# Head of the expert search: both token tiles together, parts evicted in pairs, and the next two heads' products ahead of the rest of the first search

## The chip, the cores and the metric

The kernel runs on one core of one Trainium2 chip. The metric is the device time of one execution in microseconds (us); lower is better. The core has a matrix engine (TensorE, PE in the rows), a vector engine (VectorE, DVE), a scalar engine (ScalarE, ACT), GpSimd (POOL), a queue engine (SyncE, SP) and 16 DMA engines. Each engine runs its own instructions in program order and waits on semaphores for the others.

## The reference, cut to what matters

Three blocks run one after the other on x of 256 tokens by 1024 channels, in float32. The second block ends in a product-key expert layer ("peer"), and the change is in its head. For each token and each of 8 heads a query of two 128-wide halves is scored against 128 sub-keys per half. The best 16 of each half form 256 candidate sums, and the best 16 of these name rows of a table: 16 rows for each of 8 heads and 256 tokens.

```
h2 = rmsnorm_2(x, norm2_g[l]) * (1.0 + sc2) + sh2
x = x + g2 * peer(h2, peer_wq[l], peer_subkeys[l], peer_u[l], peer_v[l])

q = (hf @ wq).reshape(T, PEER_HEADS, 2, PEER_DKEY // 2)
sc = jnp.einsum('thpd,pnd->thpn', q, subkeys)
top_v, top_i = lax.top_k(sc, PEER_TOPK)                  # 16 of 128, twice
cand_v = (top_v[:, :, 0, :, None] + top_v[:, :, 1, None, :]).reshape(T, PEER_HEADS, -1)
cand_id = (top_i[:, :, 0, :, None] * PEER_NKEYS + top_i[:, :, 1, None, :]).reshape(T, PEER_HEADS, -1)
best_v, best_j = lax.top_k(cand_v, PEER_TOPK)            # 16 of 256
ids, gates = take_along_axis(cand_id, best_j), softmax(best_v)
a = einsum('td,ted->te', xb, u_tab[ids]); w = gates * gelu(a)
y = einsum('te,ted->td', w, v_tab[ids])
```

The third block that follows (a long convolution and a mixture of experts) needs the whole x that the second block gives.

## The kernel before, in words

The 256 tokens are two tiles of 128 (t = 0, 1). A step n of the expert layer handles one table row per token of one tile: 256 steps, 128 for each tile, 16 for each head. For a step, GpSimd issues an indirect DMA (`refill`) that gathers 128 rows of 2048 floats, u and v side by side, 1 MiB. VectorE forms the dot of u with the token (`dot`), ScalarE makes the weight and a diagonal matrix from it (`weight`), and TensorE adds the weighted v into PSUM (`add`); then the buffer is free and takes the next gather. At the start there are 12 buffers (three in `E0`, four in `G0`, four in `G1`, and the first of `E0` last). A gather needs the ids of its rows, so the first one waits for the first search.

Float32 products are made of three TensorE passes over parts in a shorter format (`mm3`: high by high, low by high, high by low). Weights come by a ring of five 512 KB slots that SyncE fills in order. For each slot ScalarE writes the high part (`whi`) and VectorE the low part (`wlo`), into three buffers of the pool `split_p`; `get` hands out the next pair, and with `k.still` set it splits just one item when none is left. A slot is filled again once its `wlo` is written.

The head of `peer`: the last products of the attention's output projection end, `x_add` adds them to x in four 128 by 512 pieces (the second half g = 1 with its squares on ScalarE), the rows are normalised (`xn`), transposed on TensorE, scaled and shifted into `hfull`, and split into `hT` (high `hT3h`, low `hT3l`). In the kernel before this is done one tile at a time: `norm_rows(0)`, `transposed_rows(0)`, then the products and scores of head 0 for tile 0 (`first_scores(0)`), then `transposed_rows(1)`. Behind these, `quick` finds the best 8 rows of head 0 from the best 8 of each half; `pump(n)` makes n of the 13 pieces into which `choose` cuts the search of one head. `tokens(t)` transposes the tokens back for the dots. `rest` makes the products of heads 3 to 7 between the steps. `heads["ready"]` is the last head whose scores are there. When `rest` is through, `weights_done` swaps the 12 big buffers for 8 others; once all searches are done, four buffers in the tile `early` are added.

The order of the instructions on each engine is that of the code, written by hand; there is no planner.

Of the kernel before, what the change touches and what calls it, by code (L numbers as in the profile page):

```python
# [11 lines left out]
F32 = mybir.dt.float32  # L12
# [5 lines left out]
ALU = mybir.AluOpType  # L18
# [21 lines left out]
class K:  # L40
# [59 lines left out]
    def _process(self, wait=False, lower=None):  # L100

        nc, i = self.nc, self.done
        self._load(i + 1)
        raw, f = self.raw.pop(i), self.items[i][1]
        self.done += 1
        if f is not None:
            f(raw)
            return
        hi = self.split_p.tile([128, 1024], F32R, name="whi")
        lo = self.split_p.tile([128, 1024], F32R, name="wlo")  # L110
        nc.scalar.activation(hi, raw, AF.Copy)  # L111
        self.parts.append((hi, lo))
        if wait:
            return lambda: nc.vector.tensor_sub(lo, raw, hi)
        (lower or nc.vector).tensor_sub(lo, raw, hi)  # L115

# [705 lines left out]
def block2(k, mod, M):  # L822
# [150 lines left out]
    def x_add(g, r, ps):  # L973
        for t in range(2):
            y = sm.tile([128, 512], F32, name="s2", bufs=3)
            nc.vector.scalar_tensor_tensor(y, ps[t], rg[g][:, t:t + 1], g1[:, r * 512:r * 512 + 512], op0=ALU.mult,
                                           op1=ALU.mult)
            xs = x[:, t, r * 512:r * 512 + 512]
            (nc.vector if g and not t else nc.gpsimd).tensor_add(xs, xs, y)
            if g:  # L980
                k.square(t, r, junk)
# [38 lines left out]
    k._process()  # L1020
# [10 lines left out]
def peer(k, mod, pA, normed_at):  # L1031
# [37 lines left out]
    v2 = tk.tile([128, 2], F32, name="vm2")  # L1069

    def norm_rows(t):
        v = v2[:, t:t + 1]
        nc.vector.tensor_add(v, k.ss[:, 0, t:t + 1], k.ss[:, 1, t:t + 1])
        nc.vector.tensor_scalar(v, v, 1.0 / 1024, 1e-6, op0=ALU.mult, op1=ALU.add)
        nc.vector.tensor_scalar_mul(xn[:, t], x[:, t], k.rsqrt(tk, v, 1, f"m2{t}"))

    def transposed_rows(t, warm=0):

        u = slice(t * 128, t * 128 + 128)
        ps = [k.mm() for _ in range(2)]  # L1080
        k.keep_warm(ps[0], warm)
        for c in range(8):
            nc.tensor.transpose(ps[c // 4][:, c % 4 * 128:c % 4 * 128 + 128], xn[:, t, c * 128:c * 128 + 128], k.ident)

        def lower(q):
            c4 = slice(4 * q, 4 * q + 4)
            nc.vector.tensor_sub(hT[1][:, c4, u], hfull[:, c4, u], hT[0][:, c4, u])

        for q in range(2):
            for j in range(4):  # L1090
                c, src = 4 * q + j, ps[q][:, j * 128:j * 128 + 128]
                if j % 2:
                    nc.scalar.activation(hfull[:, c, u], src, AF.Identity, scale=normed_at[0](c), bias=normed_at[1](c))
                else:
                    nc.vector.tensor_scalar(hfull[:, c, u], src, normed_at[0](c), normed_at[1](c), op0=ALU.mult,
                                            op1=ALU.add)
            nc.scalar.activation(hT[0][:, 4 * q:4 * q + 4, u], hfull[:, 4 * q:4 * q + 4, u], AF.Copy)
            if q:
                lower(0)
        lower(1)  # L1100

    def cols_of_rows(w, t, out):

        for c in range(8):
            k.mm3(out, [z[:, c * 128:c * 128 + 128] for z in w], [z[:, c, t * 128:t * 128 + 128] for z in hT], c == 0,
                  c == 7)
# [5 lines left out]
    def half_products(r, ts=(0, 1)):  # L1112
        q, ps = q3, k.mm()
        for n in range(2):
            for t in ts:
                nc.tensor.matmul(ps[:, t * 256 + n * 128:t * 256 + n * 128 + 128], q[:, n, t * 128:t * 128 + 128],
                                 subk[:, n * 128:n * 128 + 128], start=True, stop=True)
        for t in ts:
            nc.scalar.activation(sc[t][:, 2 * r:2 * r + 2], ps[:, t * 256:t * 256 + 256], AF.Copy)

    def first_scores(t):

        u = slice(t * 128, t * 128 + 128)
        p = k.mm()[:, 0:256].rearrange("p (n t) -> p n t", n=2)
        for i in range(2):
            cols_of_rows(first[i], t, p[:, i])
        nc.scalar.activation(q3[:, :, u], p, AF.Copy)
        half_products(0, (t,))


    norm_rows(0)
    transposed_rows(0, warm=44)
    k._process()
    norm_rows(1)
    first = [k.parts.pop(0) for _ in range(2)]
    first_scores(0)
    transposed_rows(1)


# [203 lines left out]
    def choice(n):  # L1343
# [3 lines left out]
        if n == 132:  # L1347
            finish(0)
        refill()


    quick()
    refill()
    tokens(0)
    first_scores(1)
    pump(13)
    refill()
    for r in (1, 2):
        k.later(half_scores, r, k.pair(hT))
    k.settle()  # L1360
    k.settle()
    heads["ready"] = 2
    pump(13)
    refill()
# [32 lines left out]
    tiles = rest()  # L1397
    ahead(0)
    ahead(1)
    for n in range(N):  # L1400
        choice(n)
        if pr is None or n % 4 != 3:
            pump(1)
        refill()

        if tiles is not None:
            if n % 7 == 1 and n < 70:
                next(tiles)
            elif n % 7 in (3, 5) and n > 7:
                k.settle()  # L1410
                if n % 14 == 12:
# [1056 lines left out]
```

## Time and profile before

| | |
|---|---|
| device time, median of 3 runs | 2510.76 us (2506.67, 2510.76, 2510.79) |
| profiled execution: device time / span | 2506.08 us / 2504.3 us |
| TensorE busy (share of the span) | 2067.5 us (83%) |
| VectorE busy | 1281.8 us (51%) |
| ScalarE busy | 773.0 us (31%) |
| GpSimd busy | 320.9 us (13%) |
| DMA, bytes and mean rate | 861.30 MB, 344 GB/s |
| of it by GpSimd's queue (the gathers) | 268.45 MB |

The span is the time from the first to the last instruction of the profiled execution, and 1.8 us lie around it. A busy share is a mean over all three blocks, whose limits differ, so what a change in one stage is worth is read from the rows of that stage.

### The profile page before, as it was taken

The page shows a single profiled execution, that of the slowest core. Times are in us where ns is not written, and L with a number is a line of the kernel's source. Part 1 is how long each engine was busy: PE and PEld are TensorE (multiplying, and loading weights), DVE is VectorE, ACT ScalarE, POOL GpSimd, SP SyncE. Part 2 cuts the span into 40 slices and gives each one's busy share as a digit, 9 for nine tenths or more (in the row PEclk, how much of TensorE's full clock was granted, in tenths as well). Part 3 has the DMA queues.
Part 4 walks back from the last instruction along what each step waited for, and adds up shares of the span by engine and source line. Part 5 has one row for each costly group of instructions (what it writes and reads, how often), then busy time and mean ns, then how long its engine had stood idle before and what let it go on. Part 6 is the DMA issues. An engine that isn't in the chain of part 4 may idle for free. (4 is left out here: it accounts for less than half of the span.)

```text
span 2504.3 us, 30432 instructions
## 1 busy us (share of the span) xinstructions
PE 2067.5 (83%) x11288; PEld 1223.2 (49%) x11288; DVE 1281.8 (51%) x2507; ACT 773.0 (31%) x1670; POOL 320.9 (13%) x314
## 2 busy tenths in 40 slices
PE   9999999999889978988858999877776676666776
PEld 8789899788755523443423997311211111111121
DVE  8987789877678758877845887100000000000001
ACT  5754444446345545554433433000000000000000
POOL 0100000000234333333323230000000000000000
PEclk9999999999699999999999999988788887987788
DMA  7767688775399999999997358999999999999997
GB/s 261 237 213 255 209 303 304 256 249 177 117 397 419 419 419 419 406 420 421 420 419 291 119 169 311 408 418 417 417 417 418 417 417 418 417 417 418 417 417 290
DMA packets 176308, 861.30 MB, mean 344 GB/s; under 512 B 29992, under 2 KB 35296, under 8 KB 107296
## 3 DMA queue, kind: packets, MB, share of 16 engines
q1 hardware_dynamic: 125872, 578.19, 60.1%
q0 software_dynamic: 36864, 268.45, 25.9%
q10 hardware_dynamic: 13424, 12.72, 1.6%
q8 instruction: 89, 1.46, 0.2%
q14 instruction: 59, 0.48, 0.1%
HBM read 858.19 MB, written 1.10 MB: 343 GB/s over the span
## 5 line engine op out<-in xcount | busy, mean ns | idle before, releaser
L115 DVE TENSOR_TENSOR wlo<-ring,whi 128x1024 fp32r<-128x1024 f32 x224 | 277.5, 1243 | 103.7 <-ACT whi L111 102.3
L2110 DVE TENSOR_TENSOR xe<-mm,m 128x256 f32<-128x256 f32 x15 | 6.4, 425 | 604.5 <-PE mm L2108 604.5
L111 ACT ACTIVATE whi<-ring 128x1024 fp32r<-128x1024 f32 x228 | 239.3, 1055 | 163.4 <-PE mm L162 46.1
L2152 PE MATMUL mm<-K,xe 128*32 128x512 f32 x864 | 150.8, 688 | 83.0 <-DMA K<-in_moe_w_dram 82.9
L2152 PE MATMUL mm<-we,xe 128*32 128x512 f32 x864 | 143.7, 758 | 83.2 <-DMA we<-in_moe_w_dram 82.8
L161 PE MATMUL mm<-hTh,whi 128*128 128x256 f32 x608 | 174.8, 287 | 0.8 <-DVE hTl L309 0.8
L163 PE MATMUL mm<-hTh,wlo 128*128 128x256 f32 x608 | 172.8, 284 | 0.1
L162 PE MATMUL mm<-hTl,whi 128*128 128x256 f32 x608 | 172.4, 284 | 0.0
L2173 ACT ACTIVATE he<-mm 128x512 f32<-128x512 f32 x16 | 9.5, 597 | 451.0 <-PE mm L2152 451.0
L1313 ACT ACTIVATE dots<-dots 128x1 f32<-128x1 f32 x256 | 51.7, 202 | 292.1 <-DVE rowsS L1302 67.6
L1324 PE MATMUL ys<-rowsS,diag 128*128 128x512 f32 x240 | 115.3, 621 | 28.9 <-ACT diag L1316 28.8
L2189 ACT ACTIVATE heT<-mm 128x512 f32<-128x512 f32 x16 | 9.6, 597 | 379.9 <-PE mm L2187 369.6
L2255 POOL TENSOR_TENSOR x<-x,zT 128x512 f32<-128x512 f32 x1 | 1.6, 1557 | 963.7 <-ACT x L2254 963.7
L2152 PEld LDWEIGHTS mm<-K,xe 128*32 128x32 f32 x864 | 22.5, 115 | 209.9 <-DMA K<-in_moe_w_dram 194.6
L2219 DVE TENSOR_TENSOR ye<-mm,px_m 128x512 f32<-128x512 f32 x16 | 11.1, 692 | 210.5 <-PE mm L2213 210.5
L161 PEld LDWEIGHTS mm<-hTh,whi 128*128 128x128 f32 x608 | 115.7, 190 | 4.7 <-issue 2.9
L2152 PEld LDWEIGHTS mm<-we,xe 128*32 128x32 f32 x864 | 20.7, 119 | 199.0 <-DMA we<-in_moe_w_dram 179.7
L162 PEld LDWEIGHTS mm<-hTl,whi 128*128 128x128 f32 x608 | 115.3, 190 | 0.6
L163 PEld LDWEIGHTS mm<-hTh,wlo 128*128 128x128 f32 x608 | 115.3, 190 | 0.3 <-DVE wlo L115 0.3
L375 DVE SCALAR_TENSOR_TENSOR mod<-ring,mod_t,mod 128x1024 f32<-128x1024 f32 x84 | 111.2, 1324 | 0.0
L1324 PE MATMUL ys<-early,diag 128*128 128x512 f32 x172 | 84.4, 628 | 27.4 <-ACT diag L1316 27.4
L1316 ACT ACTIVATE diag<-ident,dots 128x128 f32<-128x128 f32 x256 | 102.8, 402 | 12.5 <-PE ys L1324 4.4
(556 smaller groups left out, 4821.4 us busy)
## 6 DMA issues: line engine op xcount, KB each, us to landing
we<-in_moe_w_dram SPq DMA_DIRECT2D x160, 1024.0 KB
K<-in_moe_w_dram SPq DMA_DIRECT2D x122, 1024.0 KB
ring<-in_moe_w_dram SPq DMA_DIRECT2D x100, 512.0 KB
K<-in_moe_w_dram SPq DMA_DIRECT2D x84, 512.0 KB
ring<-in_w_in_dram SPq DMA_DIRECT2D x48, 512.0 KB
ring<-in_ada_w_dram SPq DMA_DIRECT2D x48, 512.0 KB
ring<-in_mod_w_dram SPq DMA_DIRECT2D x48, 512.0 KB
ring<-in_w_qkv_dram SPq DMA_DIRECT2D x24, 512.0 KB
```

What stands on the lines that cost most here:

```text
L111: nc.scalar.activation(hi, raw, AF.Copy)
L115: (lower or nc.vector).tensor_sub(lo, raw, hi)
L161: nc.tensor.matmul(out, lhs[0], rhs[0], start=start, stop=False)
L162: nc.tensor.matmul(out, lhs[0], rhs[1], start=False, stop=False)
L163: nc.tensor.matmul(out, lhs[1], rhs[0], start=False, stop=stop)
L375: nc.vector.scalar_tensor_tensor(z, raw, th[:, ch:ch + 1], z, op0=ALU.mult, op1=ALU.add)
L1313: nc.scalar.activation(g, a, AF.Gelu)
L1316: nc.scalar.activation(diags[n], k.ident, AF.Copy, scale=w)
L1324: nc.tensor.matmul(ys[-1][:, 512 * j:512 * j + 512], d, rows[n][1][:, 1024 + 512 * j:1536 + 512 * j], start=n % 128 == 0, stop=n % 128 == 127)
L2152: nc.tensor.matmul(p[32 * j:32 * j + 32], xe[:, c], w[j], start=c == 0, stop=c == 7)
L2189: nc.scalar.activation(heT, p, AF.Copy)
L2219: nc.vector.tensor_mul(ye, p, m5)
```

## The change

The head handles all 256 tokens at once. `x_add` gives the piece t = 1 to VectorE and t = 0 to GpSimd (before it was the other way round). One `rms_x` serves both tiles; the 16 transposes fill four PSUM banks, and each eviction takes a part of 256 columns where it took 128. The low and high splits are written out in pairs of parts. The two weight items of head 0 are split in two steps: `uppers(2)` lets ScalarE write both high parts early, and `lower()` puts each low part on VectorE at a chosen place. Head 0's products are then one `pair` of 48 TensorE passes with 256 columns (before: 48 passes with 128 columns per tile, at two places). Behind `quick`, the products of heads 1 and 2 come first and the rest of head 0's search (`pump(13)`) after them; the search of head 1 moves into the first seven steps, two pieces a step. `rest` starts one item earlier, its scores count as ready seven steps earlier, and later seven steps of eight carry a piece of search (before: three of four).

```diff
-            (nc.vector if g and not t else nc.gpsimd).tensor_add(xs, xs, y)
+            (nc.vector if g and t else nc.gpsimd).tensor_add(xs, xs, y)
...
     k.rows_part(p3, yT, 3, 4)
-    k._process()
     k.later(x_add, 1, 1, p3)
...
+    def uppers(self, n):
+        self.lowers = [self._process(wait=True) for _ in range(n)]
+    def lower(self):
+        self.lowers.pop(0)()
...
-    norm_rows(0)
-    transposed_rows(0, warm=44)
-    k._process()
-    norm_rows(1)
-    first = [k.parts.pop(0) for _ in range(2)]
-    first_scores(0)
-    transposed_rows(1)
+    k.uppers(2)
+    r = k.rms_x(tk, "m2")
+    for t in range(2):
+        nc.vector.tensor_scalar_mul(xn[:, t], x[:, t], r[:, t:t + 1])
+    ps4 = [k.mm() for _ in range(4)]
+    k.keep_warm(ps4[0], 40)
+    for c in range(8):
+        for t in range(2):
+            o = c % 2 * 256 + t * 128
+            nc.tensor.transpose(ps4[c // 2][:, o:o + 128], xn[:, t, c * 128:c * 128 + 128], k.ident)
+    def full(c, on_dve):
+        src, sc, sh = ps4[c // 2][:, c % 2 * 256:c % 2 * 256 + 256], normed_at[0](c), normed_at[1](c)
+        if on_dve:
+            nc.vector.tensor_scalar(hfull[:, c], src, sc, sh, op0=ALU.mult, op1=ALU.add)
+        else:
+            nc.scalar.activation(hfull[:, c], src, AF.Identity, scale=sc, bias=sh)
+    def upper(c):
+        nc.scalar.activation(hT[0][:, c:c + 2], hfull[:, c:c + 2], AF.Copy)
+    def lower(c):
+        nc.vector.tensor_sub(hT[1][:, c:c + 2], hfull[:, c:c + 2], hT[0][:, c:c + 2])
+    full(0, True)
+    full(1, False)
+    upper(0)
+    full(2, True)
+    k.lower()
+    full(3, False)
+    lower(0)
+    upper(2)
+    full(4, True)
+    full(5, False)
+    lower(2)
+    upper(4)
+    full(6, False)
+    full(7, True)
+    lower(4)
+    upper(6)
+    lower(6)
+    k.lower()
...
         if n == 132:
+            k.settle()
             finish(0)
...
+    k.later(half_scores, 0, k.pair(hT))
+    k.settle()
+    k.settle()
     quick()
     refill()
     tokens(0)
-    first_scores(1)
-    pump(13)
-    refill()
     for r in (1, 2):
         k.later(half_scores, r, k.pair(hT))
     k.settle()
+    pump(13)
+    refill()
     k.settle()
     heads["ready"] = 2
-    pump(13)
-    refill()
...
     tiles = rest()
+    next(tiles)
     ahead(0)
     ahead(1)
     for n in range(N):
         choice(n)
-        if pr is None or n % 4 != 3:
-            pump(1)
+        if pr is None or n % 8 != 7:
+            pump(2 if n < 7 else 1)
...
-            if n % 7 == 1 and n < 70:
+            if n % 7 == 1 and n < 60:
                 next(tiles)
-            elif n % 7 in (3, 5) and n > 7:
+            elif n % 7 in (3, 5):
                 k.settle()
-                if n % 14 == 12:
+                if n % 14 == 5:
```

The first place is VectorE between the last normalised row of the head and `quick` (its first row is L1158 `MAX` before, L1151 after; `early` is the tile that holds the scores, `hfull` and the search's scratch). Before, from the normalisation of tile 1 on:

```order
L1075 TENSOR_SCALAR early_6487<-x,rsm_6576 128x1024
L1095 TENSOR_SCALAR early<-mm,mod_sc,mc 128x128 x4
L1087 TENSOR_TENSOR hT3l<-early,hT3h 128x4x128 x2
L1158 MAX early<-early 128x8
L1159 MAX_INDEX early<-early 128x8
```

After, from the normalisation of both tiles on:

```order
L1078 TENSOR_SCALAR early_6483<-x,rsm_6497 128x1024 x2
L1089 TENSOR_SCALAR early<-mm,mod_sc,mc 128x256 x2
L114 TENSOR_TENSOR wlo<-ring,whi 128x1024
L1097 TENSOR_TENSOR hT3l<-early,hT3h 128x512
L1089 TENSOR_SCALAR early<-mm,mod_sc,mc 128x256
L1097 TENSOR_TENSOR hT3l<-early,hT3h 128x512
L1089 TENSOR_SCALAR early<-mm,mod_sc,mc 128x256
L1097 TENSOR_TENSOR hT3l<-early,hT3h 128x512 x2
L114 TENSOR_TENSOR wlo<-ring,whi 128x1024
L1151 MAX early<-early 128x8
```

Before, tile 1's evictions stood between head 0's scores of tile 0 and `quick`; after, both tiles' evictions and both weight items' low parts stand ahead of the products, and nothing stands between the scores and `quick`.

The second place is VectorE right behind `quick`, whose last row writes the eight ids. Before (the rows of the 13 pieces are cut after the first three and resume with the last two):

```order
L1176 SCALAR_TENSOR_TENSOR ids_6677<-early 128x8
L1150 MATCH_REPLACE early<-early 128x128
L1144 MAX early<-early 128x8
L1145 MAX_INDEX early<-early 128x8
...
L1216 SCALAR_TENSOR_TENSOR ids<-early 128x16
L1220 RECIPROCAL gz<-gz 128x1
L115 TENSOR_TENSOR wlo<-ring,whi 128x1024 x4
```

After:

```order
L1169 SCALAR_TENSOR_TENSOR ids_6667<-early 128x8
L115 TENSOR_TENSOR wlo<-ring,whi 128x1024 x4
L1143 MATCH_REPLACE early<-early 128x128
L1137 MAX early<-early 128x8
L1138 MAX_INDEX early<-early 128x8
...
L1209 SCALAR_TENSOR_TENSOR ids<-early 128x16
L1213 RECIPROCAL gz<-gz 128x1
L115 TENSOR_TENSOR wlo<-ring,whi 128x1024 x3
L1295 SCALAR_TENSOR_TENSOR early_6483,dots_6891<-early_6483,h_6677 128x1024 x3
```

The four low parts of the weights of heads 1 and 2 moved ahead of the rest of head 0's search, and the first dots (L1295) now follow that search and three more low parts directly; before, the search of head 1 came between.

## Rows read from the trace of the kernel before

**Rows 1.** The page: the span, and the rate of all DMA in 40 equal slices of it (62.6 us each).

```profile
span 2504.3 us, 30432 instructions
GB/s 261 237 213 255 209 303 304 256 249 177 117 397 419 419 419 419 406 420 421 420 419 291 119 169 311 408 418 417 417 417 418 417 417 418 417 417 418 417 417 290
```

**Rows 2.** Busy time by stretch (us from the span's start): length, then busy us (and instructions) of TensorE, its weight loads, VectorE, ScalarE and GpSimd, the granted TensorE clock as a share of full speed, the mean busy share of the DMA engines, and GB/s. Two stretches of 5 us: the start of the gathers, and the first time that their flow thins.

```profile
675.00:680.00 5.00, 5.00 (x24) 4.83 (x23) 4.69 (x21) 0.00 (x0) 3.88 (x4) 0.50 0.65 229
...
710.00:715.00 5.00, 5.00 (x9) 2.07 (x7) 3.52 (x13) 3.70 (x9) 0.94 (x1) 0.59 0.61 251
```

**Rows 3.** The same view, two stretches of 20 us: near the end of the gathers, and behind it.

```profile
1300.00:1320.00 20.00, 5.77 (x9) 2.61 (x10) 13.97 (x36) 6.24 (x19) 1.42 (x2) 0.66 1.04 355
...
1360.00:1380.00 20.00, 9.56 (x40) 4.94 (x38) 12.55 (x33) 7.28 (x17) 5.42 (x4) 0.91 0.18 53
```

**Rows 4.** The chain that ended last, in order of time: start, us, what. One piece of VectorE behind the gathers and the first long piece of DMA after it.

```profile
1379.71 0.82 DVE K L1684
...
1564.03 8.82 DMA K<-in_moe_w_dram
```

**Rows 5.** Instructions in order of time, GpSimd's gathers: start us, duration us, engine, line, operation, and in brackets the idle time before and what ended it. The first gather, one beside `wlo` splits, the twelfth, and the thirteenth.

```profile
674.90 1.15 POOL L1276 DMA_INDIRECT early<-in_uv_dram,ids  x1 [29.68 <-DVE early L1150]
...
686.51 1.97 POOL L1276 DMA_INDIRECT G<-in_uv_dram,ids  x1 [0.30 <-issue]
...
690.10 0.94 POOL L1276 DMA_INDIRECT early<-in_uv_dram,ids  x1 [0.37 <-issue]
713.40 0.94 POOL L1276 DMA_INDIRECT early<-in_uv_dram,ids  x1 [22.37 <-PE ys L1324]
```

**Rows 6.** Instructions in order of time, from head 0's scores of tile 0 (L1119) to the ids of all 16 rows (L1216).

```profile
664.92 0.38 ACT L1119 ACTIVATE early<-mm 128x256 f32<-128x256 f32 x1 [1.31 <-PE mm L1116]
...
670.26 0.69 DVE L1087 TENSOR_TENSOR hT3l<-early,hT3h 128x512 fp32r<-128x512 f32 x1 [0.59 <-ACT hT3h L1097]
...
670.87 0.29 DVE L1158 MAX8 early<-early 128x8 f32<-128x128 f32 x1
...
674.44 0.17 DVE L1176 SCALAR_TENSOR_TENSOR ids<-early 128x8 int32<-128x8 f32 x1
...
682.31 0.17 DVE L1216 SCALAR_TENSOR_TENSOR ids<-early 128x16 int32<-128x16 f32 x1
```

**Rows 7.** Instructions in order of time, from the last pass of the output projection (L163) to the first transposes of the head (L1083).

```profile
638.51 0.40 PE L163 MATMUL mm<-whi,hT2l 128*128 128x512 f32 x1
...
640.46 1.23 DVE L115 TENSOR_TENSOR wlo<-ring,whi 128x1024 fp32r<-128x1024 f32 x1 [3.10 <-ACT whi L111]
...
643.96 1.26 POOL L979 TENSOR_TENSOR x<-x,s 128x512 f32<-128x512 f32 x1 [5.24 <-DVE s L976]
644.00 1.23 DVE L1073 TENSOR_TENSOR vm<-ssf 128x1 f32<-128x1 f32 x1 [0.19 <-ACT junk L237]
...
647.00 0.75 DVE L1075 TENSOR_SCALAR early<-x,rsm 128x1024 f32<-128x1024 f32 x1
647.80 1.97 PE L1083 MATMUL mm<-ident,early 128*128 128x128 f32 x8 [4.09 <-DVE early L1075]
```

**Rows 8.** Groups of instructions by line and shape between 640 and 720 us: count, then busy us, mean ns of one, and the idle time before them with what ended it.

```profile
L115 DVE TENSOR_TENSOR wlo<-ring,whi 128x1024 fp32r<-128x1024 f32 x9 | 10.7, 1222 | 13.2 <-ACT whi L111 13.2
...
L1087 DVE TENSOR_TENSOR hT3l<-early,hT3h 128x512 fp32r<-128x512 f32 x4 | 2.7, 687 | 1.2 <-ACT hT3h L1097 1.2
...
L1097 ACT ACTIVATE hT3h<-early 128x512 fp32r<-128x512 f32 x4 | 2.5, 630 | 0.1
```

**Rows 9.** Instructions in order of time in the second block's first norm (476 to 506 us), which treats both tiles at once: the mean square (L244), both normalised tiles (L836), 15 of the 16 transposes (L296), and two scaled evictions of 256 columns on ScalarE (L317) and on VectorE (L319).

```profile
486.70 0.16 DVE L244 TENSOR_TENSOR vm<-ssf 128x2 f32<-128x2 f32 x1 [0.97 <-ACT up L237]
...
488.67 1.41 DVE L836 TENSOR_SCALAR on<-x,rsm 128x1024 f32<-128x1024 f32 x2
...
490.13 1.86 PE L296 MATMUL mm<-ident,on 128*128 128x128 f32 x15 [0.34 <-DVE on L836]
491.15 1.02 ACT L317 ACTIVATE tr_full<-mm,mc,mod_sc 128x256 f32<-128x256 f32 x2 [1.45 <-PE mm L296]
...
494.44 0.98 DVE L319 TENSOR_SCALAR tr_full<-mm,mod_sc,mc 128x256 f32<-128x256 f32 x2
```

**Rows 10.** Busy time by stretch, columns as in rows 2: where TensorE's clock fell in the head, two stretches later in the head and one in the norm of rows 9.

```profile
645.00:646.00 1.00, 0.00 (x0) 0.00 (x0) 0.86 (x5) 0.72 (x2) 0.22 (x1) 0.91 0.00 0
...
653.00:663.00 10.00, 10.00 (x47) 10.00 (x47) 4.18 (x12) 1.35 (x2) 0.00 (x0) 0.50 0.17 53
...
687.00:690.00 3.00, 3.00 (x16) 3.00 (x16) 0.67 (x1) 0.00 (x0) 2.42 (x2) 0.50 1.00 418
...
496.00:499.00 3.00, 3.00 (x14) 3.00 (x15) 2.97 (x9) 2.96 (x9) 0.00 (x0) 0.50 0.88 285
499.00:500.00 1.00, 1.00 (x10) 1.00 (x10) 0.46 (x2) 0.98 (x2) 0.00 (x0) 0.98 0.90 336
```

**Rows 11.** Instructions in order of time: two successive product passes of 256 columns at half clock and two at full clock (the distance of their starts is the price of one).

```profile
687.11 0.41 PE L161 MATMUL mm<-hT3h,whi 128*128 128x256 f32 x1
687.32 0.41 PE L162 MATMUL mm<-hT3l,whi 128*128 128x256 f32 x1
...
690.50 0.28 PE L163 MATMUL mm<-hT3h,wlo 128*128 128x256 f32 x1
690.62 0.28 PE L161 MATMUL mm<-hT3h,whi 128*128 128x256 f32 x1
```

More of the change, by code (lines that the diff above doesn't have):

```diff
@@ L1068, in peer @@
     nc.scalar.dma_start(subk, a["subk"])
[L1069 to L1106, printed above, removed]
+    k.uppers(2)
[8 more added lines that the diff above has]
+            nc.tensor.transpose(ps4[c // 2][:, o:o + 128], xn[:, t, c * 128:c * 128 + 128], k.ident)
@@ L1110, in half_scores, with half_products @@
         k.later(half_products, r)
-    def half_products(r, ts=(0, 1)):
+    def half_products(r):
         q, ps = q3, k.mm()
         for n in range(2):
-            for t in ts:
+            for t in range(2):
                 nc.tensor.matmul(ps[:, t * 256 + n * 128:t * 256 + n * 128 + 128], q[:, n, t * 128:t * 128 + 128],
                                  subk[:, n * 128:n * 128 + 128], start=True, stop=True)
-        for t in ts:
+        for t in range(2):
             nc.scalar.activation(sc[t][:, 2 * r:2 * r + 2], ps[:, t * 256:t * 256 + 256], AF.Copy)
[L1121 to L1128, printed above, removed]
-    norm_rows(0)
-    transposed_rows(0, warm=44)
-    k._process()
-    norm_rows(1)
-    first = [k.parts.pop(0) for _ in range(2)]
-    first_scores(0)
-    transposed_rows(1)
     ids, gates = {}, {}
```

## The prediction

> **What bounds the kernel now.** I read the page first, for the rate of the DMA over the span [rows 1]. The head of the expert search lies in the slice that begins at 626 us: 117 GB/s, the lowest of all. From 689 to 1315 us every slice shows 397 to 421 GB/s: there the gathers run, and the DMA engines are the bound. The times by stretch say when this flow begins and ends: in 675 to 680 us the DMA share is 0.65, so the flow starts at about 676.7 us [rows 2], and in 1360 to 1380 us it is down to 53 GB/s [rows 3]. Behind it the chain of waits goes over VectorE and TensorE until the weights of the mixture of experts take over at 1564 us [rows 4]. So the stretch is a fixed load of bytes at a fixed rate, and what comes after waits for its end: if the flow starts x us sooner and is not interrupted, the kernel ends x us sooner. The change can win in two ways, an earlier first gather and fewer holes in the flow.
>
> Next I read what the first gather waits for. GpSimd issues it at 674.90 us, after VectorE [rows 5]. The scores of head 0 for tile 0 are being copied at 664.92 us, so they are there at 665.3; but `quick` starts only at 670.87, because VectorE, in program order, has the evictions of tile 1 ahead of it (the last is the low split at 670.26) [rows 6]. That is 5.6 us lost to order. `quick` to first gather takes 674.90 - 670.87 = 4.0 us.
>
> Last, the holes. The twelfth gather goes out at 690.10, and the thirteenth not before 713.40: all 12 buffers are full and the first dot waits for the search of head 1 [rows 5]. In 710 to 715 us the DMA share is 0.61, a hole of 0.39 x 5 = 2.0 us [rows 2].
>
> **The change, part by part.** I follow the chain from the last pass of the output projection, at 638.9 us [rows 7], up to which the order is the same but for the swap in `x_add`.
>
> *Split taken out of the way.* Before, VectorE does a `wlo` from 640.46 to 641.7 that waited for ScalarE, with the last `x_add` behind it [rows 7]. Now the last `x_add` starts at about 639.0. Before, 2.3 us pass from 641.7 to the mean square of tile 0 (644.00). That add of 128 x 1 then takes 1.23 us, as long as GpSimd's add beside it (1.26 us) [rows 7]. Now both tiles' squares are waited for, so I take 3.1 us, with bounds of 2.3 and 2.3 + 1.26: the mean square starts at 642.0. The two high parts on ScalarE lie beside the normalisation.
>
> *Both tiles at once.* The first norm of the block shows this form: from mean square to both normalised tiles 486.70 to 490.08, 3.4 us [rows 9], so 645.4 here. Fifteen transposes take 1.86 us, a bank of four 0.5 us; with a hop evictions start at 646.2.
>
> *Evictions in pairs.* On VectorE: four parts at 0.49 us (two in 0.98) [rows 9], four low splits at 0.687, two `wlo` at 1.222 [rows 8]: 2.0 + 2.7 + 2.4 = 7.1 us, so 653.3 us without a wait. ScalarE has four parts at 0.51 [rows 9] and four high splits at 0.63 [rows 8], 4.6 us, interleaved. I add 1.2 us of mutual waits: the second `wlo` ends at 654.5.
>
> *Products.* 48 passes; about half run before 654.5 as parts come in, 24 remain. A pass of 256 columns costs 0.21 us at a granted clock of 0.50 and 0.12 at 1.00 [rows 11]. A pass of 128 columns cost the same 0.21 at half clock (47 in 10 us) [rows 10]; so doing both tiles at once adds nothing to the path, and a whole set of 48 disappears later. The end is 657.4 at full clock and 659.6 at half. Copy, sub-key products and copy of the scores took 2.3 us (663.0 to 665.3) [rows 6, 10] for one tile at half clock; for two I estimate 3.9, and 2.6 at full clock. `quick` then starts at 660.0 or 663.5, against 670.87: 10.9 or 7.4 us earlier. Which clock it is the trace doesn't settle. It fell to 0.50 at 645.8 while TensorE was idle [rows 10], and the new head leaves TensorE mostly idle from 643.3 to about 648. In the norm of rows 9 it was 0.50 until 499.0, then 0.98 [rows 10]. I take the middle, 9.1 us.
>
> *Gathers beside `wlo`.* Behind `quick` there now stand four `wlo` on VectorE, the first three back to back, where small search steps stood. A gather issued beside such splits at 686.51 took 1.97 us, against 0.94 to 1.15 [rows 5]. I take 1.0 us of delay for the flow, with bounds 0 (only the first gathers meet them) and 3.7 (GpSimd is locked out for three times 1.222) [rows 8]. The Trainium skill (SBUF — State Buffer, Who interferes with whom) says that an operation with two SBUF inputs contends with GpSimd's reads and infers that writing descriptors needs the other side, so it would not stall a gather. By that the term would be 0 and the sum 1.0 us better; the long gather speaks against it, so the row goes in.
>
> *Rest of head 0's search, moved behind the next products.* It is hidden if ids 8 to 15 come before eight gathers have run. A gather is 1.05 MB, 2.5 us at 419 GB/s, and three ring slots of 0.52 MB come between: at half clock the flow runs from about 670.4 to 694. The search ends after `quick` (667.5), a `wlo`, 48 passes at 0.21, a copy, a high and a low part (together 14.4 us) and the search itself, 674.6 to 682.5, so 7.9 us [rows 6]: 690, and a gather lands its first bytes 1.8 us after issue (674.90 to 676.7). That leaves 2 us; at full clock 7. So it costs nothing.
>
> *Dots sooner, head 1 in the loop.* The first dot follows three more `wlo` at 690 to 695 us, when the twelfth gather has 10 us to run: the hole of 2.0 us goes. Rows 16 on need head 1, whose 13 pieces now lie among nine dots, some 21 to 25 us of VectorE: 711 to 719. Sixteen gathers and eight slots last until 717 to 720. I take 0, with a bound of 3 us lost.
>
> *The later edits* (searches done sooner, `rest` seven steps earlier, `settle` before `finish`) move work under a flow that is full [rows 1], so they cost nothing while it lasts. The one thin place is the loads for the third block near 1300 us (355 GB/s) [rows 3]; they come some steps later in the order: 0, bounds 2 either way.
>
> **Sum.** -9.1 + 1.0 - 2.0 = -10.1 us. On the profiled run's own 2506.1 us that gives 2496.0. The timed runs lie at 2506.7 and, twice, 2510.8; on the median it gives 2500.7. I name the middle, 2498.
>
> **Rivals.**
> *The clock is up for the products.* Then `quick` starts at 660.0, 1.8 us better than I take, and without a delay of the gathers 1.0 more: -12.9 us, 2495 by the same middle. For it: the clock rose in the norm of rows 9 soon after products began. Against: it stayed at 0.50 through ten fully busy microseconds from 653 to 663, with passes of 128 columns [rows 10]. The Trainium skill (TensorE: Matmul & The Clock Gate, What's actually happening) says that activity releases the throttle; the trace agrees for the passes of 256 columns and disagrees for those of 128.
>
> *The queue runs dry.* If the second eight ids or those of head 1 come late, the flow stops until they do; each us late is a us lost. A clock that falls in the pause before head 1's products, and the bounds above (3.7 - 1.0, and 3), take 5.7 us: -4.4, 2504. For it: the margins of 2 us at half clock. Against: at full clock 7.
>
> *Nothing gained.* If the flow were paced by something other than its bytes, an earlier start would be given back: 2508.5, the level of the runs between. The full plateau speaks against it [rows 1].
>
> *Slower: head 1's search starves the gathers.* Before, it was done ahead of the first dot; now the refill stops at row 16 until nine dots and 13 pieces are through. Each dot waits for its gather, and a step that waits holds the pieces behind it. It decides against the change from 10.1 us late: ids after about 730 us; at 737 the kernel takes 2515. Against: the dots find their first rows landed.
>
> **Chances.** Forecast 0.52, clock up 0.18, dry queue 0.17, nothing gained 0.07, slower 0.06. The measurement of this kernel tells 0.2%, 5 us, from no change. Faster by more than that: the first two and half of the third, 0.79; same 0.15; slower 0.06. The range goes from 2491 (clock up, no delay, on the level of 2506) to 2507 (dry queue, on the level of 2511).
>
> **What would show it.** `quick` should start between 660 and 664 us, VectorE having no evictions between the scores and it; the first gather 4 us later; no stretch from there to 1300 below a DMA share of 0.9; the thirteenth gather before 700; the fall behind the flow about 10 us before 1360. The forecast is wrong if the evictions wait for each other longer than 1.2 us, if the gathers beside the four `wlo` take 2 us each, or if the DMA share falls between the eighth and ninth or the sixteenth and seventeenth gather.

## The result, and the profile after

| kernel | median us (5 runs) | ratio to the kernel before, 95% interval |
|---|---|---|
| before | 2510.11 | |
| changed | 2494.69 (2491.28 to 2497.73) | 0.9946 [0.9935, 0.9957] |

The change makes the kernel faster by 0.54%, 13.6 us [10.8, 16.3]; the two medians lie 15.4 us apart. The profiled execution took 2495.38 us; that of before took 2506.08.

The page of the changed kernel, the span and the rate of all DMA in 40 slices (62.3 us each), answers to [rows 1]:

```profile
span 2493.6 us, 30332 instructions
...
GB/s 262 239 211 255 208 295 307 249 256 184 177 418 420 420 418 415 414 417 406 414 418 281 114 158 334 417 418 417 416 417 418 417 417 418 417 417 418 417 417 287
```

The slice of the head (the eleventh) has risen from 117 to 177 GB/s: the gathers start earlier in it. Next, stretches of the changed kernel, columns as in [rows 2]: the products of head 0, the start of the gathers, the place of the old hole, and the end of the flow.

```profile
640.00:660.00 20.00, 15.39 (x116) 13.52 (x115) 12.07 (x31) 9.29 (x17) 1.28 (x1) 1.00 0.22 63
...
665.00:670.00 5.00, 4.40 (x20) 4.40 (x21) 2.82 (x3) 0.00 (x0) 4.27 (x3) 0.50 0.69 215
710.00:715.00 5.00, 5.00 (x13) 2.13 (x13) 4.90 (x17) 2.98 (x12) 2.66 (x3) 1.00 1.01 415
...
1345.00:1350.00 5.00, 3.84 (x9) 1.25 (x8) 2.40 (x4) 1.80 (x6) 0.00 (x0) 1.00 0.99 408
1350.00:1355.00 5.00, 3.98 (x9) 1.37 (x9) 2.46 (x4) 2.06 (x7) 0.00 (x0) 1.00 0.17 38
```

The granted clock is 1.00 from 640 to 660 us, where before it fell to 0.50 behind 645 us [rows 10]; the hole at 710 is gone (415 GB/s against 251 [rows 2]); the flow ends at about 1350.5. The instructions in order of time, first of the head and then GpSimd's first and thirteenth gathers, answer to [rows 5] and [rows 6]:

```profile
643.36 0.16 DVE L251 TENSOR_TENSOR vm<-ssf 128x2 f32<-128x2 f32 x1 [0.99 <-ACT junk L244]
...
655.48 0.39 PE L170 MATMUL mm<-hT3h,wlo 128*128 128x256 f32 x1
...
660.67 0.29 DVE L1151 MAX8 early<-early 128x8 f32<-128x128 f32 x1 [5.25 <-ACT early L1130]
...
664.71 1.86 POOL L1269 DMA_INDIRECT early<-in_uv_dram,ids  x1 [22.90 <-DVE ids L1169]
666.88 1.76 POOL L1269 DMA_INDIRECT early<-in_uv_dram,ids  x1 [0.30 <-issue]
...
694.95 0.94 POOL L1269 DMA_INDIRECT early<-in_uv_dram,ids  x1 [3.63 <-DVE early L1143]
```

VectorE no longer stands between scores and `quick` (first row L1151): it waits 5.25 us for the scores. The thirteenth gather follows 30 us behind the first (38.5 before).

The work upstream drifts by some us from one profiled execution to the next: the last pass of the projection starts at 638.51 in the profile of before [rows 7], at 640.33 in this one. So I compare places in time relative to that start. The end of the flow is taken by bytes: the end of the last stretch of 5 us with over 400 GB/s, and the bytes of the next two at 420. A ratio in the table is to the kernel before on the chip of that run, where its median was 2507.0 to 2508.4 us for all rows from d0 on.

| kernel | median us | ratio, 95% interval | mean square | `quick` | first gather | 13th gather | flow's end |
|---|---|---|---|---|---|---|---|
| before | 2510.11 | | 5.5 | 32.4 | 36.4 | 74.9 | 722.7 |
| changed | 2494.69 | 0.9946 [0.9935, 0.9957] | 3.0 | 20.3 | 24.4 | 54.6 | 710.1 |
| changed, again (d0) | 2496.18 | 0.9954 [0.9940, 0.9968] | 3.0 | 20.3 | 24.4 | 54.1 | 710.2 |
| a1: no filling passes | 2495.30 | 0.9946 [0.9933, 0.9960] | 3.0 | 21.1 | 25.2 | 53.8 | 711.0 |
| d3: passes of 128 columns | 2510.41 | 1.0012 [1.0003, 1.0021] | 3.0 | 35.2 | 39.2 | 68.8 | 724.7 |
| a2: split put back | 2495.56 | 0.9951 [0.9937, 0.9964] | 6.2 | 23.7 | 27.7 | 57.6 | 712.8 |
| b0: before, `quick` ahead | 2511.05 | 1.0013 [1.0004, 1.0023] | 5.5 | 26.4 | 30.4 | 77.8 | 725.6 |
| b1: before, dots sooner | 2503.45 | 0.9984 [0.9975, 0.9993] | 5.5 | 32.4 | 36.4 | 70.2 | 718.5 |
| a3: first search ahead | 2499.04 | 0.9964 [0.9951, 0.9978] | 3.0 | 20.4 | 24.4 | 61.1 | 712.1 |
| c3: dots late | 2494.14 | 0.9950 [0.9937, 0.9964] | 3.0 | 20.4 | 24.4 | 62.8 | 708.6 |
| d2: dots and `rest` late | 2494.57 | 0.9951 [0.9937, 0.9964] | 3.0 | 20.4 | 24.4 | 59.9 | 709.8 |
| c2: late edits back | 2497.22 | 0.9954 [0.9940, 0.9968] | 3.0 | 20.3 | 24.4 | 51.1 | 709.0 |
| c1: passes in order of operands | 2492.27 | 0.9942 [0.9928, 0.9955] | 3.0 | 17.7 | 21.8 | 51.7 | 707.4 |
| d1: c1 again | 2491.72 | 0.9937 [0.9924, 0.9951] | 3.0 | 17.7 | 21.8 | 50.4 | 708.8 |

(Columns from the fourth on: us behind the start of the projection's last pass.) In the profile `quick` is 12.0 us earlier and the flow's end 12.6. What follows the flow's end takes the same as before, 2493.6 - 1350.45 = 1143.1 us against 1143.0. The repetition d0 was expected within 1 us; it took 1.5 us longer, with its places in the trace within 0.5 us of the first. The two profiles of one other kernel, c1 and d1, differ by 1.4 us in the flow's end, so a difference of that size tells nothing there.

### The profile page after: what moved, and what is told of

It is laid out like the page before. It is cut to its first block, busy times and chain, and to the rows that moved or that the text cites. A ratio compares the mean times of both kernels' runs of the same rounds, so it can differ in the third digit from the quotient of the medians.

```text
span 2493.6 us, 30332 instructions
## 1 busy us (share of the span) xinstructions
PE 2064.8 (83%) x11236; PEld 1213.6 (49%) x11236; DVE 1277.5 (51%) x2501; ACT 773.8 (31%) x1667; POOL 320.1 (13%) x314
## 5 line engine op out<-in xcount | busy, mean ns | idle before, releaser
L1317 PE MATMUL ys<-rowsS,diag 128*128 128x512 f32 x248 | 124.1, 639 | 18.4 <-ACT diag L1309 18.3
L1317 PE MATMUL ys<-early,diag 128*128 128x512 f32 x188 | 91.9, 625 | 22.7 <-ACT diag L1309 22.6
```

Of the source, the lines that this page charges most:

```text
L1317: nc.tensor.matmul(ys[-1][:, 512 * j:512 * j + 512], d, rows[n][1][:, 1024 + 512 * j:1536 + 512 * j], start=n % 128 == 0, stop=n % 128 == 127)
```

## The experiments

**The clock: is it the filling, or the passes?** The forecast had left the clock open and taken a middle. Two runs. a1 takes the 40 filling passes away:

```diff
-    k.keep_warm(ps4[0], 40)
```

> The changed kernel without the 40 filling passes ahead of the 16 transposes of the head; everything else is as in the changed kernel. Theory (the clock at 1.00 through the head is what made the first gather come earlier than forecast): without the filling the granted clock falls to 0.50 behind the projection, as in the kernel before, and is still there for the 48 products; they and the copies behind them take 3.5 us more, quick starts at about 664.2 instead of 660.7, and the time is 3.5 us longer (2498.2 by the median of the changed kernel). Rival (the chain is VectorE's and ScalarE's, the clock matters to neither the transposes nor the last products): quick at 660.7 to 661.5, time within 1 us.

Stretches of a1, columns as in [rows 2]:

```profile
645.00:650.00 5.00, 3.95 (x17) 3.56 (x17) 3.69 (x7) 2.04 (x5) 0.00 (x0) 0.50 0.00 0
650.00:655.00 5.00, 3.21 (x20) 2.60 (x20) 3.75 (x7) 2.66 (x5) 0.00 (x0) 0.99 0.36 107
```

The clock does fall to 0.50, for the transposes and the first passes, and is back at 0.99 while the products wait for parts. `quick` moves by 0.8 us and the time by nothing that can be measured. The theory that the filling keeps the products fast falls. d3 leaves the filling out like a1 and halves the columns of each of head 0's passes, which doubles their number:

```diff
-    k.keep_warm(ps4[0], 40)
...
-    k.later(half_scores, 0, k.pair(hT))
+    p = k.mm().rearrange("p (n t) -> p n t", n=2)
+    for n in range(2):
+        w = k.get()
+        for t in range(2):
+            u = slice(t * 128, t * 128 + 128)
+            for c in range(8):
+                k.mm3(p[:, n, u], [z[:, c * 128:c * 128 + 128] for z in w], [z[:, c, u] for z in hT], c == 0, c == 7)
+    k.later(half_scores, 0, p)
```

> The changed kernel without the filling passes, and with head 0's 48 products of 256 columns done as 96 of 128 columns (each half, then each tile). Theory (as in the kernel before, where ten fully busy microseconds of 128-column passes left the granted clock at 0.50, while 256-column passes raised it here within 5 us even without the filling): the clock stays at 0.50 through the products, the passes cost 0.21 us each, and quick starts about 9 us later than with 256 columns and no filling (21.1 behind the projection's last pass), at 29 to 31; time 8 to 10 us longer. Rival (columns don't matter, the time since the engine became busy does): the clock rises within 5 us of the products' start, and quick is less than 3 us later.

Two stretches of d3, and from its instructions in order of time one of the 128-column passes, the start of `quick` and the first gather:

```profile
650.00:666.00 16.00, 16.00 (x76) 16.00 (x76) 1.77 (x2) 0.00 (x0) 0.00 (x0) 0.50 0.11 34
...
671.50:672.00 0.50, 0.44 (x4) 0.20 (x2) 0.47 (x3) 0.50 (x1) 0.00 (x0) 1.00 0.00 0
```

```profile
662.34 0.41 PE L170 MATMUL mm<-hT3h,wlo 128*128 128x128 f32 x1
...
671.09 0.29 DVE L1150 MAX8 early<-early 128x8 f32<-128x128 f32 x1 [19.32 <-ACT early L1129]
...
675.12 1.87 POOL L1268 DMA_INDIRECT early<-in_uv_dram,ids  x1 [37.72 <-DVE ids L1168]
```

TensorE is busy for all of 16 us and the clock stays at 0.50. A pass costs 16.00 / 76 = 0.21 us, as much as one of 256 columns at that clock [rows 11]. `quick` is 14.1 us later than in a1 (my 9 had been added up wrongly: 48 more passes at 0.21 are 10.1, and 48 at 0.21 instead of 0.12 are 4.3, together 14.4). The time is 14.2 us above d0 on the same chip. With narrow passes, all 96 of them ahead of `quick`, and everything else of the change in place but the filling, which a1 shows to be worth nothing that can be measured, the kernel is back at the time of before. So what the change is worth hangs on the width of the passes, by their number and by the clock at which they ran. The Trainium skill (TensorE: Matmul & The Clock Gate, What's actually happening) says that activity releases the throttle; here 16 us of full activity did not, as in [rows 10]. The clock of d3 rises between 671.0 and 671.5 us, behind the sub-key products and the transposes for `tokens`, which are 128 columns wide too, but in float32 and not over parts. What it is in the narrow passes over parts that goes with the low clock, d3 does not separate.

**The split out of the way.** a2 puts the first weight item's split back ahead of the last `x_add`:

```diff
+    k._process()
     k.later(x_add, 1, 1, p3)
...
-    k.uppers(2)
+    k.uppers(1)
...
     full(2, True)
-    k.lower()
     full(3, False)
```

> The changed kernel with the first weight item of head 0 split where the kernel before did it, ahead of the last addition to x (so only one high part lies early on ScalarE, and one low part fewer among the evictions). Theory: the last addition waits for ScalarE's high part and then 1.23 us for the low part, which makes the mean square 2.0 to 2.8 us later; one low part fewer among the evictions gives 1.2 back, so quick starts 0.8 to 1.6 us later and the time is as much longer (2495.5 to 2496.3). Rival (the low part among the evictions lies in a wait and costs nothing there): quick 2.8 us later, time 2.8 us longer.

From a2's instructions in order of time, the split, the mean square and the transposes:

```profile
639.91 1.23 DVE L115 TENSOR_TENSOR wlo<-ring,whi 128x1024 fp32r<-128x1024 f32 x1 [1.95 <-ACT whi L111]
...
644.76 0.16 DVE L251 TENSOR_TENSOR vm<-ssf 128x2 f32<-128x2 f32 x1 [0.99 <-ACT junk L244]
...
648.25 3.46 PE L1085 MATMUL mm<-ident,early 128*128 128x128 f32 x15 [0.19 <-DVE early L1079]
```

The mean square is 3.2 us later, the transposes lie at half clock (3.46 us against 1.86), and the low part fewer gives back little, some 0.7 us (3.2, and 0.8 for the half clock by a1, less 3.3): `quick` is 3.3 us later and the flow's end 2.7, the rival's figure. The timed median, 0.9 above the first and 0.6 below the second measurement of the changed kernel, can't tell 2.7 us from 0; I go by the places in the trace.

**Is an early first gather enough?** b0 is the kernel before with `quick` moved ahead of tile 1's transposes:

```diff
     first_scores(0)
-    transposed_rows(1)
...
     quick()
     refill()
+    transposed_rows(1)
     tokens(0)
     first_scores(1)
```

> The kernel before with quick and its gathers moved ahead of the transposes and evictions of tile 1; nothing else. Theory (an early first gather alone is not enough: 12 buffers hold about 31 us of flow, and the first dot, which frees the first, comes behind the searches of heads 0 and 1 as before): the first gather goes out at about 669.3 instead of 674.9, but the first dot stays at about 706 to 708, so the hole at the end of the first twelve grows from 2.0 to about 7.6 us, and the time is that of the kernel before within 1.5 us. Rival (the first gather alone sets the end, as the term of the forecast puts it): 5.6 us shorter.

Its first, twelfth and thirteenth gathers, and the stretches in between:

```profile
667.54 1.15 POOL L1275 DMA_INDIRECT early<-in_uv_dram,ids  x1 [23.69 <-DVE ids L1175]
...
684.05 0.94 POOL L1275 DMA_INDIRECT early<-in_uv_dram,ids  x1 [0.30 <-issue]
714.95 0.94 POOL L1275 DMA_INDIRECT early<-in_uv_dram,ids  x1 [29.96 <-PE ys L1323]
```

```profile
705.00:715.00 10.00, 4.11 (x5) 1.85 (x6) 9.09 (x26) 5.52 (x17) 0.06 (x1) 0.53 0.09 35
715.00:720.00 5.00, 5.00 (x29) 3.75 (x28) 4.26 (x4) 2.60 (x3) 2.49 (x2) 0.92 0.68 224
```

The first gather comes 6.0 us earlier, the first buffer is free 2.9 us later, and the hole takes more than was won: by bytes ((420 - 35) x 10 + (420 - 224) x 5) / 420 = 11.5 us, against 3.3 before (below). The flow's end is 2.9 us later, as the first free buffer is. The time is 0.13% longer, so the theory held. What counts is by how much the distance from the first gather to the first free buffer exceeds what the buffers and the ring slots hold.

**Dots sooner, in the kernel before and in the new one.** b1 gives the kernel before only the search of head 1 in the loop:

```diff
     heads["ready"] = 2
-    pump(13)
-    refill()
...
-            pump(1)
+            pump(2 if n < 7 else 1)
```

> The kernel before with only this part of the change: the search of head 1 moves from ahead of the first dot into the first seven steps, two pieces a step. Theory (the parts add up): the first gather stays where it is, the thirteenth goes out before the twelfth has landed, the hole of 2.0 us at 710 to 715 goes, and the time is 2.0 us shorter than before. Rival (the pieces between the dots make the ids of rows 16 on late): a hole opens between the sixteenth and seventeenth gather, and the time is that of before or up to 3 us longer.

The kernel before (its stretch from 710 us is in [rows 2]) and then b1:

```profile
715.00:720.00 5.00, 5.00 (x30) 3.76 (x29) 4.93 (x11) 1.96 (x5) 1.71 (x1) 1.00 0.93 311
```

```profile
710.00:715.00 5.00, 5.00 (x30) 3.76 (x30) 4.86 (x14) 1.42 (x6) 1.17 (x2) 1.00 1.01 414
715.00:720.00 5.00, 5.00 (x12) 2.01 (x11) 4.90 (x13) 4.81 (x12) 1.67 (x2) 1.00 1.02 416
```

The hole goes, and the time falls by 0.16% [0.07%, 0.25%], 4.0 us; the flow's end is 4.2 us earlier. My 2.0 us came from one stretch's busy share. By bytes, over both, the hole before was (420 - 251 + 420 - 311) x 5 / 420 = 3.3 us.

In the changed kernel I put things back in three ways. a3 does the rest of head 0's search directly behind `quick`, c3 the search of head 1 ahead of the first dot, d2 that and a later start of `rest`:

```diff
     tokens(0)
+    pump(13)
+    refill()
     for r in (1, 2):
         k.later(half_scores, r, k.pair(hT))
     k.settle()
-    pump(13)
-    refill()
```

> The changed kernel with the rest of head 0's search put back directly behind quick, ahead of the products of heads 1 and 2; quick, evictions, products of head 0 and the search of head 1 in the loop stay. Theory (the order behind quick is worth only the stretch of the first gathers, the buffers cover the rest): the first gathers take 0.95 to 1.15 us instead of 1.86 and 1.76 and the flow begins up to 1.0 us earlier; the low parts and the first dot come some 8 us later than in the changed kernel, at about 700, which is still before the twelfth gather lands; time 0 to 1 us shorter. Rival (the products of head 1 come so late that the ids of rows 16 on or the first dots stop the flow): a stretch with a DMA share below 0.9 between 690 and 730, and 1 to 4 us longer.

c3:

```diff
     heads["ready"] = 2
+    pump(13)
+    refill()
...
-            pump(2 if n < 7 else 1)
+            pump(1)
```

> The changed kernel with the search of head 1 put back ahead of the first dot (13 pieces in one go, then one piece a step). Theory (the buffers hold about 34 us of flow, until 700): the first dot comes some 8 us later, the thirteenth gather goes out at about 703 instead of 695, and the flow has a hole of 3 to 4 us at 701 to 706; in return the ids of rows 16 on are there early; time 3 us longer. Rival (the early start carries the gain alone): no hole, time unchanged.

d2 is c3 with, in addition:

```diff
-    next(tiles)
     ahead(0)
...
-            if n % 7 == 1 and n < 60:
+            if n % 7 == 1 and n < 70:
                 next(tiles)
-            elif n % 7 in (3, 5):
+            elif n % 7 in (3, 5) and n > 7:
                 k.settle()
-                if n % 14 == 5:
+                if n % 14 == 12:
```

> The changed kernel with the search of head 1 ahead of the first dot and, in addition, the products of heads 3 to 7 begun at step 1 again instead of ahead of the first dot (with the scores counted seven steps later, as before). Theory (the twelve buffers alone hold the flow until about 700; with the search alone put back it lasted because two more ring slots were filled ahead, 2.5 us of flow): the hole returns, 2 to 3 us at 700 to 706, and the time is 2 to 3 us longer than the changed kernel. Rival (the hole does not depend on the slots): no stretch with a share below 0.97, time as with the search alone put back (2494).

Two stretches of a3, then one each of c3 and d2:

```profile
715.00:720.00 5.00, 5.00 (x15) 2.37 (x14) 4.86 (x19) 2.98 (x12) 2.81 (x3) 1.00 0.61 202
720.00:725.00 5.00, 5.00 (x29) 3.68 (x28) 3.95 (x10) 2.42 (x6) 2.17 (x3) 1.00 0.99 388
```

```profile
700.00:705.00 5.00, 5.00 (x26) 3.33 (x25) 3.52 (x13) 3.18 (x9) 1.88 (x2) 1.00 1.03 419
```

```profile
700.00:705.00 5.00, 5.00 (x31) 3.80 (x30) 4.93 (x10) 1.40 (x4) 1.43 (x2) 1.00 0.94 356
```

a3: the rival held. The products of heads 1 and 2, some 8 us later, leave the flow short between the sixteenth and the seventeenth gather, by bytes (420 - 202 + 420 - 388) x 5 / 420 = 3.0 us, and the end is 1.9 us later; the timed difference to the two measurements of the changed kernel is 4.4 and 2.9 us. c3: the rival held, no hole, though the thirteenth gather is 38.4 us behind the first, as far as in the kernel before. d2: a dip of (420 - 356) x 5 / 420 = 0.8 us where 2 to 3 were expected, and no loss.

The difference to the kernel before is in the ring. Twelve gathers are 30.0 us of flow at 420 GB/s, and each ring slot is 1.25 us of flow that needs no gather buffer. SyncE's loads between the first and the thirteenth gather, in the kernel before, in c3 and in d2:

```profile
685.42 11.00 SPq L96 DMA_DIRECT2D ring<-in_wq_dram  x4
```

```profile
664.11 33.44 SPq L96 DMA_DIRECT2D ring<-in_wq_dram  x7
```

```profile
663.20 11.33 SPq L96 DMA_DIRECT2D ring<-in_wq_dram  x4
```

That is 35.0, 38.8 and 35.0 us of flow for distances of 38.5, 38.4 and 35.5 us: 3.5 us too little, enough, and 0.5 too little, where the holes measured 3.3, 0 and 0.8 us. b0, with 4 slots for 47.4 us, comes out 12.4 short, measured 11.5. The changed kernel has 7 slots for 30.2 us, 8.6 to spare. So in the new head the earlier dots are cover, not gain. With 4 slots c3 would be 3.4 us short; that is an estimate from this sum, and no run shows it.

**The later edits.** c2 has the lines of d2 (without those of c3) and, in addition:

```diff
         if n == 132:
-            k.settle()
             finish(0)
...
-        if pr is None or n % 8 != 7:
+        if pr is None or n % 4 != 3:
```

> The changed kernel with the late edits taken back: the products of heads 3 to 7 start at step 1 again, their scores count as ready seven steps later, three steps of four carry a piece of search, and no settle stands ahead of the first tile's end. Theory (they lie under a full flow): no change within 1 us, and the thin stretches near 1180 (406 GB/s at a share of 0.99) and 1320 us (372 GB/s) stay. Rival (they cost the 1.6 us of the 14.0 that are lost between the head and the end of the flow): 1.6 us shorter, and the stretches look as in the kernel before.

The flow's end is 709.0, 1.1 us before that of the changed kernel, and the time is longer than both its measurements, by up to 2.5 us: no change that can be told. The thin stretches of the changed kernel near 1180 us go, against what I expected (418 GB/s from 1160 to 1220), but others come at 1080:

```profile
1080.00:1140.00 60.00, 49.86 (x147) 25.00 (x146) 46.08 (x109) 31.84 (x90) 18.28 (x20) 0.89 0.98 392
```

That is 4.0 us of flow, so the later edits aren't the cause that the flow thins.

**A better order for head 0.** After the last low part 22 of the 48 passes still follow (655.48 to 658.2), though most of their operands had long been there. c1 and its repetition d1 run the passes as parts come in, with the evictions, the low parts and the two copies moved to match (the diff is cut to the passes):

```diff
+    def head0():
+        ps = [k.mm() for _ in range(2)]
+        w = [k.get() for _ in range(2)]
+        def go(z, part, pair, start=False, stop=False):
+            for c in (2 * pair, 2 * pair + 1):
+                for n in range(2):
+                    nc.tensor.matmul(ps[n][:, 0:256], w[n][z][:, c * 128:c * 128 + 128], hT[part][:, c],
+                                     start=start and c == 0, stop=stop and c == 7)
+        go(0, 0, 0, start=True)
...
+        go(0, 1, 3, stop=True)
+        nc.scalar.activation(q3[:, 0], ps[0][:, 0:256], AF.Copy)
+        nc.vector.tensor_copy(q3[:, 1], ps[1][:, 0:256])
```

> A further step on the changed kernel: the 48 passes of head 0 run in the order in which their operands come (both halves of a part together, in two PSUM banks, what needs the two low parts of the weights spread between) instead of one half after the other; a bank of transposes is evicted by one engine where possible; the first weight's low part lies before the evictions; the two banks of the query are copied by ScalarE and VectorE side by side, and the sub-key products of tile 0 come first. Theory (the head's chain is now bound by the order of the passes: in the changed kernel 2.8 us of passes still follow the last low part, and VectorE idles 5.25 us ahead of quick): the last low part comes at about 653.5 instead of 655.4, only 4 passes follow, and the copies take 0.8 us less, so quick starts 4 to 5 us earlier, at 15.3 to 16.3 us behind the last pass of the projection instead of 20.3; the first dot moves with it, the flow ends as much earlier, and the time is 4 to 5 us shorter (2490). Rival (the first dots or the ids of rows 16 on are now set by something that does not move with quick, such as weights that come by the ring): the flow starts 4 us earlier and a hole of 4 us opens before 720; time unchanged.

> The further step on the head (passes of head 0 in the order in which their operands come) once more, to be compared with the changed kernel on the same chip. Theory (quick 2.6 us earlier, carried to the end as in its first run): 2.5 us shorter than the changed kernel here. Rival (its first time was a draw of the runs' spread): within 1 us of it.

From d1's instructions in order of time, the second low part of the weights, the last passes, and `quick`:

```profile
648.86 1.22 DVE L114 TENSOR_TENSOR wlo<-ring,whi 128x1024 fp32r<-128x1024 f32 x1
...
653.47 1.12 PE L1126 MATMUL mm<-hT3l,whi 128*128 128x256 f32 x8
...
656.56 0.29 DVE L1177 MAX8 early<-early 128x8 f32<-128x128 f32 x1 [1.51 <-ACT early L1156]
```

`quick` is 2.6 us earlier in both runs, not 4 to 5: from 650.6 to 654.5 TensorE now works without a pause, so I take its own passes for the bound. The flow's end is 2.7 us earlier in c1 and 1.4 in d1. On the same chip d1 takes 4.5 us less than the changed kernel (five runs each, 2490.35 to 2492.68 against 2493.02 to 2497.91, without overlap); the trace accounts for 1.4 to 2.7 of that, the rest isn't explained. It beats both kernels, by 0.63% [0.49%, 0.76%] over the kernel before.

## Why the prediction was right, step by step

The time (2494.7 and 2496.2 for 2498) lies in the range, and the mechanism held: fixed bytes at a fixed rate, an earlier start, a closed hole, and an unchanged rest behind the flow. Of the signs it named, four held: the first gather 4.0 us behind `quick`, the thirteenth ahead of 700, no stretch of 5 us up to 1300 below a DMA share of 0.9 (the lowest is 0.93, at 1180), and an earlier fall, by 12.6 us for about 10. One did not: counted from the projection's last pass as in the profile of before, `quick` starts at 658.9, ahead of the 660 to 664 that were named. The terms:

- *First gather earlier, forecast 9.1, measured 12.0.* This is the mis-sized term. Its other parts held within half a us each (mean square forecast 3.5 us behind the start of the projection's last pass, measured 3.0; from the first eviction to the end of the second low part 8.0 us for 8.3), and together they gave 1.1 us of the 2.9. What failed is "I take the middle" of two clocks, the other 1.8 us: the rival with the clock up was right. I read the clock as something that the filling and the idle stretch decide; a1 and d3 show that with 256-column passes it came up without the filling, and with 128-column passes it did not in 16 busy us. [Rows 10, 11] pointed to it: the stretch that stayed low for 10 us holds 128-column passes, and at the two places where the clock rose, 499 and 690 us, 256-column passes run, though they too had been at 0.50 before.
- *Gathers beside `wlo`, forecast 1.0, measured 0.* The two long gathers were there (1.86 and 1.76 us), but the flow did not wait for them. Counted back from 670 us by its bytes, it starts 27.1 us behind the projection's last pass (670 - 215 / 420 x 5 - 640.33); in a3, whose first gathers take 1.15 and 0.94 us, 27.2 (670 - 351 / 420 x 5 - 638.57). In the same count d0, c2, c3 and d2, which have the long gathers too, lie at 26.8 to 27.7, so a delay of 1.0 us in the mean would show. The stretch of a3:

```profile
665.00:670.00 5.00, 0.00 (x0) 0.00 (x0) 4.72 (x15) 0.60 (x3) 3.78 (x5) 0.50 0.94 351
```

What the Trainium skill infers (SBUF — State Buffer, Who interferes with whom), that such an operation leaves the writing of descriptors alone, fits the flow here, and not the gather's own duration (1.86 us for 1.15).
- *The hole, forecast 2.0, measured 3.3* by bytes (b1). My reason, earlier dots, is right for the kernel before (b1) and not needed in the new one (c3, d2), where ring slots fill the gap.
- *Rest of head 0's search moved: 0.* It costs nothing, as forecast, but the term left out that it is needed: with the opposite order (a3) the ids of rows 16 on come late and 2 to 3 us are lost. *Later edits: 0, held* (c2), within what the times can tell.
- *Not forecast: some 2.5 us lost on the way.* 12.0 + 3.3 would be 15.3; the flow's end moved by 12.6. From 720 us to its end the flow lacks 6.7 us of 420 GB/s before and 9.2 after (5 us times the sum of 1 - rate / 420 over stretches of 5 us, up to the last with over 400). All runs with the new head lack 8.2 to 10.3, before, b0 and b1 6.0 to 7.0; c2, with the later edits back, is at 8.8. The cause is open. The largest piece, in the kernel before and then in the changed one:

```profile
1160.00:1220.00 60.00, 50.90 (x146) 23.36 (x145) 44.79 (x105) 31.42 (x91) 21.58 (x24) 0.97 1.01 421
```

```profile
1160.00:1220.00 60.00, 51.84 (x168) 27.30 (x167) 49.12 (x120) 33.04 (x93) 20.89 (x22) 0.94 1.01 405
```

So the sum came out closer than its terms: 2.9 and 1.3 us more gain and 1.0 us of delay that wasn't there make 5.2 us, and this loss took 2.5 of them back. That the two errors go against each other is luck, not insight.

## What to carry to other kernels

Where a flow of transfers is the bound, price an edit ahead of it by three places: when the first transfer goes out, when the first buffer is free again, and what other bytes can fill the time between; an earlier start alone (b0) was worth nothing, because the first buffer came free no earlier. Read a hole in GB/s over all its stretches, not by the busy share of one. When two ways of doing the same products differ in width, look up at which clock each width runs elsewhere in the trace before a middle is taken: here the two cases of the forecast lay 3.5 us apart, and the narrow passes of d3 cost 14.

## What the runs showed of the hardware that was not expected

- 76 of d3's 96 passes of 128 columns kept TensorE busy without a pause from 650 to 666 us at a granted clock of 0.50 and cost 0.21 us each, the price of a 256-column pass at that clock; the same work in 256 columns had 0.99 to 1.00 from 650 on and 0.12 us a pass, with pauses (a1). In d3 the clock came up between 671.0 and 671.5 us, behind 128-column products and transposes in float32.
- Two first gathers that took 1.86 and 1.76 us on GpSimd, for 1.15 and 0.94 in a3, did not delay the bytes of the flow: it starts 27.1 us behind the projection's last pass, 27.2 in a3.
- The DMA engines can show a busy share of 1.01 at 405 GB/s as well as at 421 (60 us each): the share alone doesn't tell that a flow is at its rate.
